# A matmul with leaky ReLU by Strassen's seven products: t2's load issued from another queue, and the last product's two row tiles in two PSUM banks

## The chip, the cores and the metric

The kernel runs on one core of one Trainium2 chip. The metric is device time in microseconds (us); lower is better. Inputs and outputs lie in DRAM.

## The reference

```python
def setup_inputs():
    m, k, n = 4096, 4096, 4096
    return {"a": randn(m, k) as float32, "b": randn(k, n) as float32, "alpha": float32(0.01)}

def reference(a, b, alpha):
    x = np.matmul(a, b)
    return np.where(x > 0, x, alpha * x)
```

## The kernel before

**Tiling.** The output is cut into 4 row groups `g` and 4 column pairs `j`. One pair `(g, j)` is a region of 1024 x 1024 outputs: a 2 x 2 arrangement of blocks of 512 x 512, each 4 row tiles `mt` of 128 rows. The inputs are taken as float16, and the inner dimension is halved too, so that A and B of a region are 2 x 2 blocks (`a11` to `a22`, `B(half, nt, k)`, where `k` counts the two tiles of a half). The first region `(0, 0)` is computed with plain products (line 279). The other 15 are the list `regions`, in the order of the loop at line 715; in groups 1 to 3 the first is `j == CACHED`, column pair 2.

**Seven products.** Each of these regions is computed with seven products instead of eight, by sums of blocks (Strassen's scheme in Winograd's form). `s1` to `s4` are sums of blocks of A (`sum_a`, line 539), `t1` to `t4` sums of blocks of B (`b_sum`, line 569). The products, in order, are a11 x B11, a12 x B21, s2 x t2, s3 x t3, s1 x t4 (written over t2's tiles), a22 x (a sum written over B21), s4 x B22. The text numbers them from 0. Products 0 to 4 are 64 matmuls of 512 columns each (line 734), into four PSUM banks: `y` and `z` in turn. In ten regions the last two products are done by seven quarter products each (`quarter_product`, line 684, 16 matmuls of 256 columns). `keep` (line 747) copies four banks into float32 tiles `c` on ScalarE, `add` (line 864) adds banks to them on VectorE (DVE), and `leave` applies leaky ReLU on DVE (line 307) and stores each tile with a DMA that SyncE (SP) issues (line 869). ScalarE and DVE also measure squares of the inputs (lines 227 to 260), from which the end of the kernel decides whether the result may stand; a branch with a plain product in bfloat16 follows for inputs for which it may not.

**What is kept in DRAM.** A region with `j == CACHED` in groups 2 and 3 finds its sums t2 and t3 ready: group 1's region of the same columns has left them in DRAM tensors `kept_t` (`move_t`, line 500). t3 is loaded during the region before, from `fetch_unit`; t2 is loaded in the region itself, behind product 0, into the tiles with the tag `b11`, the same tiles that held B11 for product 0. Product 2 reads t2. Some loads of B in these regions come from a float16 copy (`kept`, line 510); all other loads of A and B are issued by GpSimd's queue (lines 130 and 513).

**Order.** The instructions of each engine stand in the order in which the code emits them (a manual schedule), with waits on semaphores put in where one engine's work needs another's. Each engine, SP's DMA queue and ScalarE's DMA queue among them, takes its instructions in order; a DMA issue that waits holds back what follows it on its engine. In the first region of groups 2 and 3, SP's order around the change is: four stores of the region before (`leave(kept_c, 0, 1)`), two stores of s2 to DRAM (`keep_s2`, line 707), the two loads of t2 (line 500), four stores of this region's first block. ScalarE's order there is: four copies of the region before (line 1034), four copies of product 0's banks (line 747), later four copies of product 2's. DVE's is: the sums s1 and s2 (line 539), leaky for the stores of the region before, the sums s3 and s4, `add` for product 1.

The place of the load, in the loop over regions:

```python
_, u1 = keep(y, side)
for k in ks:
    if g > 1 and j == CACHED:
        t = have_b[i, k, 0] = b_pool.tile([P, KC, NT], DT, name="b", tag="b11")
        move_t("t2", t, k, False)
        continue
```

**The end.** The seventh product of the last region is `seventh_at_the_end`. Its seven quarter products go partly onto the banks `y`, and partly into two further banks, `one` and `other`. `one` holds two row tiles side by side, 256 columns each. Three quarter products accumulate in it: after the first and the second, ScalarE copies it out (lines 835 and 838); the third, the last of the kernel, is ordered by row tile (`by_row=True`), and DVE adds each half of the bank to both halves of an output tile (line 855), applies leaky, and the tile is stored (line 859, and line 1039 in the branch).

Of the kernel before, what the change touches and what calls it, by code (L numbers as in the profile page):

```python
# [8 lines left out]
P = 128  # L9
DT = mybir.dt.float16  # L10
# [14 lines left out]
KC = 8  # L25
# [5 lines left out]
NT = 512  # L31
# [4 lines left out]
CACHED = 2  # L36
# [10 lines left out]
def kernel(  # L47
# [16 lines left out]
    nc = tc.nc  # L64
# [10 lines left out]
    b_pool = ctx.enter_context(tc.tile_pool(name="bblk", bufs=2))  # L75
# [12 lines left out]
    x = small_pool.tile([P, 8], FP32, name="x")  # L88
# [114 lines left out]
    def new_bank(i):  # L203
        return psum_pool.tile([P, NT], FP32, name="ps", tag=f"ps{i}")
# [98 lines left out]
    part = {}  # L303
    stores = []

    def leaky(t):
        nc.vector.scalar_tensor_tensor(t, t, alpha, t, op0=MULT, op1=MAX if alpha <= 1 else MIN)  # L307
# [27 lines left out]
    for what, i, *more in order:  # L335
        if what == "a":
            r, tiles = more
            k = slice(r * rw, (r + 1) * rw)
# [43 lines left out]
    banks = {}  # L382
# [62 lines left out]
    for i in range(1, len(steps)):  # L445
        t, h, u, first, last = steps[i]
# [16 lines left out]
        t, h, u, first, last = steps[i]  # L463
        if first:
            banks = {(mt, nt): new_bank(2 * mt + nt) for mt in range(MT) for nt in range(2)}
# [18 lines left out]
    kept = dram_pool.tile([2, KU * KW, NT], DT, name="kept")  # L484
# [10 lines left out]
            for k in ks:  # L495
                fetch_unit(i, 2 * half + k, nt)

    def move_t(name, t, k, out):
        ends = kept_t[name][k], t.rearrange("p c n -> p (c n)")
        nc.sync.dma_start(*(ends if out else ends[::-1]))  # L500

    def fetch_unit(i, u, nt):
        g, j = regions[i]
# [15 lines left out]
    have_b = {(0, u, nt): bt[1, u, nt] for u in range(2) for nt in range(2)}  # L519
# [105 lines left out]
    HALF = NT // 2  # L625
# [5 lines left out]
    def a_quarter(t):  # L631
        return t.rearrange("p (c m e) -> p c m e", m=HALF, e=2)

    def b_quarter(t):
        return t.rearrange("p (c n) -> p c n", n=HALF)

    def quarters_of_b(i, half, nt):
        return {(k, n): have_b[i, 2 * half + k, nt][:, :, n * HALF:(n + 1) * HALF]
                for k in range(2) for n in range(2)}

    def quarters_of_a(g, name):
        return {(h, k): operand(g, name, k)[:, :, h * HALF:(h + 1) * HALF, :] for h in range(2) for k in range(2)}
# [32 lines left out]
        for n in which:  # L675
            queue.dma_start(to[n], kept_q[name][n - 1])

    def quarter_product(xq, yq, to, first=False, by_row=False):
        order = [(c, m) for c in range(KC) for m in range(2)]
        if by_row:  # L680
            order = [(c, m) for m in range(2) for c in range(KC)]
        for c, m in order:
            rows = slice(m * P, (m + 1) * P)
            nc.tensor.matmul(  # L684
                to[m], xq[:, c // 2, rows, c % 2], yq[:, c, :],
                start=first and (c, m) == (0, 0), stop=c == KC - 1, skip_group_check=True,
            )

    def into(bank):
        return [bank[:, m * HALF:(m + 1) * HALF] for m in range(2)]  # L690

    def pair(bank):
        return bank.rearrange("p (m n) -> p m n", m=2)
# [21 lines left out]
    for i, (g, j) in enumerate(regions):  # L715

        ks = (1, 0) if in_quarters else (0, 1)
# [5 lines left out]
        zbank = 4 - ybank  # L723
# [15 lines left out]
        def new_c(side):  # L739

            pairs = [c_pool.tile([P, 2, NT], FP32, name="c", tag=f"c{side}") for _ in range(2)]
            return pairs, [pairs[mt // 2][:, mt % 2, :] for mt in range(MT)]

        def keep(banks, side):
            pairs, kept = new_c(side)
            for mt in range(MT):
                nc.scalar.copy(kept[mt], banks[mt])  # L747
            return pairs, kept
# [73 lines left out]
                nc.vector.tensor_add(kept[mt], y[mt], kept[mt])  # L822
            return kept

        def seventh_at_the_end(y, one, other, tq, sq):

            pairs, kept = new_c(side)
            b = quarters_of_b(i, 1, 1)
            x = quarters_of_a(g, "s4")
            t = lambda n: b_quarter(tq[n])  # L830
            sx = lambda n: a_quarter(sq[n])
            block = lambda r, n: pairs[r][:, :, n * HALF:(n + 1) * HALF]
            onto = lambda r, n: [y[2 * r + m][:, n * HALF:(n + 1) * HALF] for m in range(2)]
            quarter_product(x[0, 0], b[0, 0], into(one), True)
            nc.scalar.copy(block(0, 0), pair(one))
            quarter_product(sx(4), b[1, 1], onto(0, 1))
            quarter_product(sx(2), t(2), into(one))
            nc.scalar.copy(block(0, 1), pair(one))
            for mt in (2, 3):
                nc.scalar.copy(kept[mt][:, HALF:], y[mt][:, HALF:])  # L840
            quarter_product(sx(1), t(1), into(other), True)
            nc.vector.tensor_add(block(0, 1), pair(other), block(0, 1))
            nc.vector.tensor_add(block(1, 1), pair(other), block(1, 1))
            quarter_product(x[0, 1], b[1, 0], onto(0, 0))
            even = nc.values_load(good[0:1, 0:1], min_val=0, max_val=1)
            add(kept[:2], y[:2])
            leave(kept[:2], 0, 1)
            quarter_product(x[1, 1], t(4), onto(1, 0))
            for mt in (2, 3):
                nc.scalar.copy(kept[mt][:, :HALF], y[mt][:, :HALF])  # L850
            quarter_product(sx(3), b[0, 1], into(one), by_row=True)
            for mt in (2, 3):
                both_halves = kept[mt].rearrange("p (h n) -> p h n", h=2)
                part = one[:, (mt - 2) * HALF:(mt - 1) * HALF]
                nc.vector.tensor_add(both_halves, part.unsqueeze(1).to_broadcast([P, 2, HALF]), both_halves)  # L855
                leaky(kept[mt])
                last = place(g, 0, mt, j, 1), kept[mt]
                if mt == 2:
                    nc.sync.dma_start(*last)
            return even, last  # L860

        def add(acc, banks):
            for to, bank in zip(acc, banks):
                nc.vector.tensor_add(to, bank, to)  # L864

        def leave(acc, h, nt):
            for mt, t in enumerate(acc):
                leaky(t)
                nc.sync.dma_start(place(g, h, mt, j, nt), t)
# [20 lines left out]
        y = [new_bank(ybank + mt) for mt in range(MT)]  # L890
# [14 lines left out]
            early.end()  # L905
        if middle:
            middle.begin()
        _, u1 = keep(y, side)
        for k in ks:
            if g > 1 and j == CACHED:  # L910
                t = have_b[i, k, 0] = b_pool.tile([P, KC, NT], DT, name="b", tag="b11")
                move_t("t2", t, k, False)
                continue
            b_sum(B(0, 1, k), B(1, 1, k), B(0, 1, k), SUB)
            if late_s2 and k == ks[0]:
                load_s2(g, ks[1], True)
            b_sum(B(0, 0, k), B(0, 1, k), B(0, 0, k), ADD)
            if g == 1 and j == CACHED:
                move_t("t3", B(0, 1, k), k, True)
                move_t("t2", B(0, 0, k), k, True)  # L920
# [32 lines left out]
        if in_quarters:  # L953
            t = x_pool.tile([P, 4, QUARTER], DT, name="q", tag="x")
            tq, sq = {2: t[:, 0], 1: t[:, 1], 4: t[:, 2]}, {4: t[:, 3]}
# [29 lines left out]
        if turning:  # L985
            new_s(g + 1, "s1")
            t = new_s(g + 1, "s2").rearrange("p k c m e -> p (k c m e)").bitcast(BF16)
            a21 = measure(i + 1, 0, 1, 0, t.rearrange("p (n w) -> p n w", n=4))
            a21.begin()
        if in_quarters:  # L990
            tq, sq = sixth_in_quarters(u2_pairs, [new_bank(zbank + mt) for mt in range(MT)], v, y, tq, sq)
# [26 lines left out]
        if in_quarters:  # L1018

            rest = y, new_bank(zbank + 3), new_bank(zbank + 2), tq, sq  # L1020
            if final:
                even, last = seventh_at_the_end(*rest)
            else:
                kept_c = seventh_in_quarters(*rest)
                fetch_b(i + 1, [(1, 1)], (1, 0))
                new_s(g, "s2")
                load_s2(g, 1)
                leave(kept_c, 0, 1)
        else:
            product(6, y, False)  # L1030
            fetch_b(i + 1, [(1, 1)], ks)
            _, kept_c = new_c(side)
            for mt in range(MT):
                nc.scalar.copy(kept_c[mt], y[mt])  # L1034
            leave(kept_c, 0, 1)
# [5 lines left out]
    with inputs.Else():  # L1041
        for m in range(M // RM):
            a_blocks = []
            for u in range(KU):
                t = a_pool.tile([P, KC // 2, RM, 2], BF16, name="a", tag=f"a{u // 2 + 1}{m % 2 + 1}")
                for mt in range(0, MT, 2):
                    to = lambda t0, t1: [t[:, :, (mt + t0) * P:(mt + t1) * P, :]]
# [4 lines left out]
            for n in range(N // NT):  # L1052
                banks = [new_bank(n % 2 * 4 + mt) for mt in range(MT)]
                cols = slice(n * NT, (n + 1) * NT)
                for u in range(KU):
                    t = b_pool.tile([P, KC, NT], BF16, name="b", tag=f"b{u // 2 + 1}{n % 2 + 1}")
                    src = b[u * KW:(u + 1) * KW, cols].rearrange("(p c) n -> p c n", p=P)
                    nc.gpsimd.dma_start(t, src)
                    for c in range(KC):
                        for mt in range(MT):  # L1060
                            nc.tensor.matmul(
                                banks[mt], a_cols(a_blocks[u], c, mt), t[:, c, :],
                                start=(u, c) == (0, 0), stop=(u, c) == (KU - 1, KC - 1),
                            )
                for mt in range(MT):
                    t = c_pool.tile([P, 2, NT], FP32, name="c", tag=f"c{side}")[:, 0]
# [38 lines left out]
```

## Time and profile before

| What | us |
|---|---|
| median of 3 runs | 1555.78 |
| lowest and highest run | 1552.80, 1559.15 |
| the profiled execution | 1562.96 |
| its span, from the first to the last instruction | 1561.10 |
| mean granted TensorE clock | 0.996 |
| TensorE (PE) busy | 1541.8 (99%) |
| DVE busy | 1154.5 (74%) |
| ScalarE (ACT) busy | 373.7 (24%) |
| HBM read and written | 369.10 MB, 98.57 MB |

The profile is of one execution. Its times are in us from the start of its span. A row of a timeline has a start, a length, an engine, a line, the operation with what it writes and reads, a count, and in brackets how long the engine sat idle before it and what released it; an engine name with a q is the queue that issues DMAs. In the rows of waits the figures are the us in total, the number of times and the longest. Rows of PE run on to the end of their last matmul's latency, so consecutive rows overlap a little.

### The profile page before, as it was taken

How to read it: one execution, taken by the hardware profiler on the slowest of the kernel's cores; microseconds unless marked ns; L12 is line 12 of the kernel's file. 1: busy time of each engine (PE TensorE's matmuls, PEld its weight loads, DVE VectorE, ACT ScalarE, POOL GpSimd, SP SyncE). 2: the span in 40 equal slices, each digit the busy share in tenths (PEclk: the TensorE clock that was granted, in tenths of full speed). 3: DMA queues.
4: the chain of work that ended last, by engine and by line, in shares of the span. 5: the costliest groups of instructions: out<-in, count | busy, mean ns of one | idle time of the engine just before them, and what ended most of it. 6: DMA issues, size and time to landing. Idle time of an engine off the chain costs nothing. (4 is left out here: it accounts for less than half of the span.)

```text
span 1561.1 us, 20714 instructions
## 1 busy us (share of the span) xinstructions
PE 1541.8 (99%) x8235; PEld 805.5 (52%) x8235; DVE 1154.5 (74%) x1315; ACT 373.7 (24%) x392; POOL 300.2 (19%) x482
## 2 busy tenths in 40 slices
PE   9999999999999999999999999999999999999997
PEld 4444444444447456474444746547444474745646
DVE  4368758777995686966798588685879668688696
ACT  2201243612100414301211141431021133051430
POOL 5541110244002011023400202012340110201100
PEclk9999999999999999999999999999999999999999
DMA  9999694999869789499987959969998794978923
GB/s 246 186 208 196 138 284 150 184 201 193 283 246 260 166 193 283 122 264 222 182 299 237 245 139 230 229 148 278 208 232 294 189 270 102 275 166 194 288 82 138
DMA packets 210092, 329.68 MB, mean 211 GB/s; under 512 B 18497, under 2 KB 155969, under 8 KB 202050
## 3 DMA queue, kind: packets, MB, share of 16 engines
q0 software_dynamic: 149376, 141.59, 57.1%
q1 hardware_dynamic: 54562, 165.31, 28.4%
q10 hardware_dynamic: 6048, 21.37, 3.7%
q8 instruction: 66, 1.08, 0.3%
q14 instruction: 40, 0.33, 0.1%
HBM read 369.10 MB, written 98.57 MB: 300 GB/s over the span
## 5 line engine op out<-in xcount | busy, mean ns | idle before, releaser
L734 PE MATMUL ps<-b,a 128*128 128x512 f16 x3200 | 696.4, 379 | 0.0
L734 PEld LDWEIGHTS <-a 128*128 128x128 f16 x3200 | 313.0, 98 | 375.7
L734 PE MATMUL ps<-b,s 128*128 128x512 f16 x2240 | 492.1, 381 | 6.6 <-DMA b<-kept_t 6.6
L734 PEld LDWEIGHTS <-s 128*128 128x128 f16 x2240 | 219.8, 98 | 273.6 <-DVE c L864 7.5
L513 POOL DMA_DIRECT2D b<-in_b_dram x184 | 136.4, 746 | 939.0 <-PE ps L734 464.0
L569 DVE TENSOR_TENSOR b<-b 128x4096 f16<-128x4096 f16 x104 | 234.8, 2286 | 94.0 <-DMA b<-in_b_dram 88.0
L747 ACT COPY c<-ps 128x512 f32<-128x512 f32 x180 | 92.6, 597 | 470.8 <-PE ps L734 408.5
L139 DVE STREAM_TRANSPOSE a<-a 128x512 uint32<-128x512 uint32 (+2 forms) x120 | 126.7, 1102 | 82.0 <-DMA a<-in_a_dram 80.5
L130 POOL DMA_DIRECT2D a<-in_a_dram x252 | 137.8, 555 | 195.8 <-DVE a L139 116.4
L307 DVE SCALAR_TENSOR_TENSOR c<-c 128x512 f32<-128x512 f32 x240 | 149.3, 681 | 3.1 <-ACT c L1034 3.0
L227 ACT ACTIVATE sq<-b 128x2048 bf16<-128x2048 f16 x64 | 119.0, 1909 | 106.0 <-DVE sq L236 90.1
L864 DVE TENSOR_TENSOR c<-ps,c 128x512 f32<-128x512 f32 x142 | 88.7, 680 | 74.0 <-PE ps L734 63.2
L684 PEld LDWEIGHTS <-q 128*128 128x128 f16 x1280 | 125.3, 98 | 14.5
L279 PE MATMUL ps<-b,a 128*128 128x512 f16 x512 | 113.1, 379 | 2.7 <-DVE part L318 1.3
L227 ACT ACTIVATE sq<-a 128x2048 bf16<-128x2048 f16 x48 | 89.0, 1908 | 101.1 <-DVE sq L236 80.0
L279 PEld LDWEIGHTS <-a 128*128 128x128 f16 x512 | 49.6, 98 | 64.2 <-issue 5.4
L684 PE MATMUL ps<-b,q 128*128 128x256 f16 x640 | 74.8, 273 | 0.0
L810 ACT COPY c<-ps 128x512 f32<-128x512 f32 x9 | 5.3, 586 | 253.1 <-PE ps L684 140.6
L763 DVE TENSOR_TENSOR c<-ps,c 128x512 f32<-128x512 f32 x80 | 52.2, 683 | 14.6 <-PE ps L684 14.6
L684 PE MATMUL ps<-q,q 128*128 128x256 f16 x480 | 57.3, 273 | 0.0
L684 PEld LDWEIGHTS <-a 128*128 128x128 f16 x480 | 47.0, 98 | 7.6
L684 PEld LDWEIGHTS <-s 128*128 128x128 f16 x480 | 46.9, 98 | 5.5
(101 smaller groups left out, 769.4 us busy)
## 6 DMA issues: line engine op xcount, KB each, us to landing
b<-in_b_dram POOLq DMA_DIRECT2D x192, 512.0 KB, 12.9
out_dram<-c SPq DMA_DIRECT2D x240, 256.0 KB, 6.2
a<-in_a_dram POOLq DMA_DIRECT2D x244, 128.0 KB, 5.4
b<-kept SPq DMA_DIRECT2D x20, 1024.0 KB, 8.3
q<-kept_qs ACTq DMA_DIRECT2D x40, 512.0 KB, 8.2
s<-kept_s SPq DMA_DIRECT2D x18, 1024.0 KB, 7.3
q<-kept_qa SPq DMA_DIRECT2D x28, 512.0 KB, 6.0
b<-kept_t SPq DMA_DIRECT2D x8, 1024.0 KB, 9.2
```

The lines of the kernel that those rows point to most:

```text
L130: nc.gpsimd.dma_start(a16[32 * q:32 * q + 32], src.rearrange("(g i) w -> i g w", i=32))
L139: nc.vector.transpose(part.rearrange("p c m e -> p c (m e)").bitcast(U32) .rearrange("p c (g i) -> p g c i", i=32), src[:, :, i * n:(i + 1 ...
L227: nc.scalar.activation(to, self.parts[n], SQUARE)
L279: nc.tensor.matmul(ps, a_cols(at[0, h, u], c, mt, (h, u) == (0, 0)), bt[0, u, nt][:, c, :], start=first, stop=last,)
L307: nc.vector.scalar_tensor_tensor(t, t, alpha, t, op0=MULT, op1=MAX if alpha <= 1 else MIN)
L513: nc.gpsimd.dma_start(t[:, c:c + 4, :], b_rows(j, u, c, 4, nt, g > 0))
L569: nc.vector.tensor_tensor(f(to), f(x0), f(x1), op)
L684: nc.tensor.matmul(to[m], xq[:, c // 2, rows, c % 2], yq[:, c, :], start=first and (c, m) == (0, 0), stop=c == KC - 1, skip_group_check=True,)
L734: nc.tensor.matmul(banks[mt], a_cols(t, c, mt, t is first_a), B(half, nt, k)[:, c, :], start=first and (k, c) == todo[0], stop=(k, c) == t ...
L747: nc.scalar.copy(kept[mt], banks[mt])
L763: nc.vector.tensor_add(block, pair(t), block)
L864: nc.vector.tensor_add(to, bank, to)
```

## The change

`move_t` gets an argument for the queue, and the two loads of t2 are issued by ScalarE's queue, ahead of the four copies that `keep` puts there, instead of by SP's. In `seventh_at_the_end` the bank `one` is replaced by two banks: each of the two row tiles has the first 256 columns of its own. The new one is `new_bank(zbank + 1)`, which the sixth product's quarters used before. The two copies of a whole bank become two copies of half a bank each, and the adds at the end read the two banks.

```diff
-    def move_t(name, t, k, out):
+    def move_t(name, t, k, out, queue=nc.sync):
         ends = kept_t[name][k], t.rearrange("p c n -> p (c n)")
-        nc.sync.dma_start(*(ends if out else ends[::-1]))
+        queue.dma_start(*(ends if out else ends[::-1]))
...
-    def quarter_product(xq, yq, to, first=False, by_row=False):
+    def quarter_product(xq, yq, to, first=False, by_row=False, banks=1):
...
-                start=first and (c, m) == (0, 0), stop=c == KC - 1, skip_group_check=True,
+                start=first and c == 0 and m < banks, stop=c == KC - 1, skip_group_check=True,
...
-        def seventh_at_the_end(y, one, other, tq, sq):
+        def seventh_at_the_end(y, one, other, tq, sq, one_more):
...
-            quarter_product(x[0, 0], b[0, 0], into(one), True)
-            nc.scalar.copy(block(0, 0), pair(one))
+            ones = [bank[:, :HALF] for bank in (one, one_more)]
+
+            def copies(n):
+                for m in range(2):
+                    nc.scalar.copy(kept[m][:, n * HALF:(n + 1) * HALF], ones[m])
+
+            quarter_product(x[0, 0], b[0, 0], ones, True, banks=2)
+            copies(0)
             quarter_product(sx(4), b[1, 1], onto(0, 1))
-            quarter_product(sx(2), t(2), into(one))
-            nc.scalar.copy(block(0, 1), pair(one))
+            quarter_product(sx(2), t(2), ones)
+            copies(1)
...
-            quarter_product(sx(3), b[0, 1], into(one), by_row=True)
+            quarter_product(sx(3), b[0, 1], ones, by_row=True)
             for mt in (2, 3):
                 both_halves = kept[mt].rearrange("p (h n) -> p h n", h=2)
-                part = one[:, (mt - 2) * HALF:(mt - 1) * HALF]
-                nc.vector.tensor_add(both_halves, part.unsqueeze(1).to_broadcast([P, 2, HALF]), both_halves)
+                nc.vector.tensor_add(both_halves, ones[mt - 2].unsqueeze(1).to_broadcast([P, 2, HALF]), both_halves)
                 leaky(kept[mt])
...
+        have_t2 = g > 1 and j == CACHED
+        if have_t2:
+            for k in ks:
+                t = have_b[i, k, 0] = b_pool.tile([P, KC, NT], DT, name="b", tag="b11")
+                move_t("t2", t, k, False, nc.scalar)
         _, u1 = keep(y, side)
         for k in ks:
-            if g > 1 and j == CACHED:
-                t = have_b[i, k, 0] = b_pool.tile([P, KC, NT], DT, name="b", tag="b11")
-                move_t("t2", t, k, False)
-                continue
+            if have_t2:
+                break
...
-                even, last = seventh_at_the_end(*rest)
+                even, last = seventh_at_the_end(*rest, new_bank(zbank + 1))
```

## The prediction

> **What bounds the kernel now.** I read the page's engine rows first, then the table of waits, then the PE, DVE and SP timelines at the place that the waits name, then the DMA view and the windows there, and last the timeline of the end.
>
> ```profile
> PE 1541.8 (99%) x8235; PEld 805.5 (52%) x8235; DVE 1154.5 (74%) x1315; ACT 373.7 (24%) x392; POOL 300.2 (19%) x482
> ```
> TensorE is the bound: only its gaps are worth anything. The table of waits has one large row of PE's (us in total, times, longest):
>
> ```profile
> PE ps L734 <- DMA b<-kept_t: 6.6, 2, 4.2
> ```
> That is product 2, s2 times t2, of the first region of groups 2 and 3. The three timelines at the first case (start, length, engine, line):
>
> ```profile
> 791.30 27.79 PE L734 MATMUL ps<-b,a 128*128 128x512 f16 x128
> 823.30 15.26 PE L734 MATMUL ps<-b,s 128*128 128x512 f16 x64 [4.21 <-DMA b<-kept_t]
> 838.39 13.98 PE L734 MATMUL ps<-b,a 128*128 128x512 f16 x64
> ...
> 809.88 2.48 DVE L307 SCALAR_TENSOR_TENSOR c<-c 128x512 f32<-128x512 f32 x4
> ...
> 810.58 2.14 SPq L869 DMA_DIRECT2D out_dram<-c  x4
> 812.81 0.89 SPq L707 DMA_DIRECT2D kept_s<-s  x2
> 813.79 2.45 SPq L500 DMA_DIRECT2D b<-kept_t  x2
> ```
> The load of t2 (L500) needs only that product 0 is done with the tile it overwrites. Product 0 began at 791.30 and lasts 13.81 us (the step between two undisturbed product starts, 777.49 and 791.30), so the k=0 tile is free at 798.2 and the k=1 tile at 805.1. But SP issues in order: t2 stands behind four stores of the region before, which wait for leaky on DVE (809.88), and behind two stores of s2. It is issued at 813.79, 15.6 us late, and shares the DMA engines with 3 MB put in just before. The DMA view from 800 to 840 us, one digit per us, and its row for t2 (last figure: us to landing):
>
> ```profile
> DMA  9995200000059999999999998997000069999600
> ...
> b<-kept_t SPq DMA_DIRECT2D x2, 1024.0 KB, 10.0
> ```
> The engines were idle from 805 to 810, ahead of that burst. The second case has the same shape:
>
> ```profile
> 1174.21 27.79 PE L734 MATMUL ps<-b,a 128*128 128x512 f16 x128
> 1204.37 15.66 PE L734 MATMUL ps<-b,s 128*128 128x512 f16 x64 [2.38 <-DMA b<-kept_t]
> 1219.87 13.98 PE L734 MATMUL ps<-b,a 128*128 128x512 f16 x64
> ```
>
> **Part 1, t2 on ScalarE's queue: what goes.** Three products should take 3 x 13.81 = 41.43 us. They took 838.39 - 791.30 = 47.09 and 1219.87 - 1174.21 = 45.66: losses of 5.66 and 4.23, 9.89 together. Of the first, 4.37 is the stall itself (823.30 against a due start of 818.93) and 1.28 follows it; of the second, 2.53 and 1.69. The second piece is the clock. In the windows just behind the stalls (the figure before the last two is the granted clock):
>
> ```profile
> 823.20:826.50 3.30, 3.20 (x9) 1.21 (x10) 3.30 (x6) 0.00 (x0) 0.00 (x0) 0.58 0.93 376
> 1204.30:1208.50 4.20, 4.13 (x12) 1.60 (x13) 4.20 (x6) 0.00 (x0) 0.00 (x0) 0.59 0.96 378
> ```
> The clock was 0.58 and 0.59 there, 1.00 after. The stall took it down, so without the stall both pieces go. The Trainium skill, page "TensorE: Matmul & The Clock Gate", section "What's actually happening", has the array fall to half clock after at least one idle window of about 3.4 us; by that the second stall, 2.4 us, would cost no clock and the sum would be 1.69 less. The trace disagrees: 0.59 behind 2.4 us.
>
> **What it adds.** ScalarE's queue gets two loads behind the copies of the region before (done 792.9) and ahead of product 0's four copies (L747, 804.67). In the built program the loads wait for product 0 and for tile loads of B that were issued before it began, nothing later. An issue on this queue takes 0.33 us (the L676 rows: 0.326 median), so k=0 goes out at 798.2, k=1 at 805.1, and the copies start about 0.8 late and end near 807.6 (in the second case 1181.1, 1188.0 and 1190.5). Behind them nothing runs on ScalarE until 837.95, and product 2 needs the copied banks at 818.93: 11 us of cover, beyond which each us would be a us of stall. Landing: the nearest rows are 4.8 to 10.7 us for L500 and up to 11.2 for the B loads beside it (L510), so k=0 lands by 809.4 (needed 818.93) and k=1 by 816.3 (needed 825.8). Cost: nothing; below nothing is excluded since no consumer starts on the copies before 818.93.
>
> What is late next? Product 2's first weight load then waits for s2 alone, which DVE ended by 809.95 (9 us early). Product 3 needs s3 (816.7) and banks emptied by DVE's L864 (823.54) at 832.7. Product 4 needs t4, from L569, which ran 835.39 to 837.67 for k=0, at 846.6; the k=1 half can only move forward. The quarters that begin at 860.4 need DVE's L646 to L656, done at 851.5. The least of these margins is 8.9 us. Loads of the next region wait on PE's own progress and move with it. Stores on SP only lose two transfers ahead of them. So the 9.89 stays gained.
>
> **Part 2, two banks at the end.** Before, both row tiles of the last quarter product shared a bank, and DVE's add for the first waited for all 16 matmuls:
>
> ```profile
> 1550.76 1.91 PE L684 MATMUL ps<-b,q 128*128 128x256 f16 x16
> 1552.78 0.69 DVE L855 TENSOR_TENSOR c<-ps,c 128x512 f32<-128x512 f32 x1 [1.19 <-PEq L1038]
> ...
> 1554.83 0.69 DVE L307 SCALAR_TENSOR_TENSOR c<-c 128x512 f32<-128x512 f32 x1
> 1555.60 0.33 SPq L1039 DMA_DIRECT2D out_dram<-c  x1
> ```
> Now it waits for the first eight: 8 x 0.109 us earlier (16 matmuls step by 1.75), 0.87. DVE is free then (its last leaky before ended at 1551.59; the add could start at 1551.91) and the copy that it needs ended at 1551.2. The chain add, leaky, add, leaky keeps its lengths, and its second add, at 1553.24, is behind PE's end. All that follows, the last store included, moves by 0.87. Added: each of two copies of 0.59 becomes two of 128x256, 0.66 a pair (L840's row): 0.07 each, under waits for PE of 2.9 us and more. The new bank was last read by the L763 that starts at 1538.72 and is done at 1539.41; its first matmul is due at 1540.39. That cover is 1 us; without it PE would lose what it is short.
>
> **Sum.** 9.89 + 0.87 = 10.76. The profiled execution took 1562.96 (span 1561.10 and 1.86 around it), and would take 1552.20. The median of the runs is 1555.78, 7.18 less than that execution, and PE's steady rate can't be where it differs: from 123.97 to 1552.67 PE lost 10.1 us against its steps, of which 9.89 are these stalls. The 7.18 came from the stalls (9.89), the head (13.5 over its steps), the tail (8.43) or the 1.86, together 33.7. None of it from the stalls: gain 10.76, 1545.0. All of it: 2.71 + 0.87 = 3.58, 1552.2. I take the proportional share, 7.18 x 9.89 / 33.7 = 2.1: gain 8.65, **1547.1**.
>
> **Rivals.**
> - **Small stalls without the profiler.** Stall length hangs on a race of DVE and DMA against PE; it differed by 1.8 us between two equal places. Then the gain is 3.58 to 7.8 and the time 1548 to 1552.2, within 0.5%. For it: the 7.18. Against: no row puts them there. 0.17.
> - **The queue doesn't matter.** If the landing were set by the 16 DMA engines, a load from another queue would land no earlier; only part 2 is left, 1554.9. Against: the idle digits from 805 to 810, and an issue 15.6 us late. The Trainium skill, page "DMA: Bandwidth & Descriptors", section "Issuing engines are not separate DMA queues", says that issuing from several engines saves only the time to initiate; here what is saved is the queue's wait before that. 0.05.
> - **Given back downstream** by a B load or sum I have as covered: half the gain, 1551. 0.04.
> - **Slower: ScalarE is held.** A load that waits on its engine holds the copies behind it. Were the wait for SP's s2 stores (issued 812.81, landing about 820 to 823), t2 would go out at 823 and land at 833: 9.7 us later than now, twice, 1575. It decides from an issue after 813.79. For it: in-order queues caused the present stall. Against: the built waits. 0.08 with lesser forms.
>
> **Numbers.** The forecast has 0.66. About 0.5% (7.8 us) is what a measurement of this kernel tells from no change. Faster by more: 0.66; within: 0.17 + 0.05 + 0.04 = 0.26; slower: 0.08. Range: 1545.0 less 3, half the 6.35 that the runs spread, is 1542; above, 1552.2 and nearly the 1554.9: 1554.
>
> **What would show it.** Right: L500 on ACT's queue at about 798 and 805 (1181, 1188); no PE wait for kept_t; product 2 on time, clock 1.00 behind it; the add at the end about 0.1 us behind the eighth of the last 16 matmuls, not behind the last. Wrong: ACT's L747 later than 817; PE waiting at product 2 for ACT or s2; a new PE wait later in the region; or all of this there and the time within 4 us of before, which would mean the stalls belonged to the profiled execution.

## The result and the profile after

| | kernel before | changed kernel |
|---|---|---|
| median of 17 runs each, us | 1557.99 | 1552.78 |
| lowest and highest run | 1552.80, 1562.46 | 1551.24, 1553.94 |
| the profiled execution | 1562.96 | 1552.24 |

The ratio of the times is 0.9966, with a 95% interval from 0.9957 to 0.9976: faster by 0.34%. The median fell by 5.2 us where 8.65 was forecast, and the profiled execution by 10.72 where the sum said 10.76. The spread of the runs shrank from 9.7 us to 2.7.

The profile after shows the first part as forecast. These are PE's rows at the two places (timeline; start, length, engine, line):

```profile
790.30 27.79 PE L734 MATMUL ps<-b,a 128*128 128x512 f16 x128
817.93 13.98 PE L734 MATMUL ps<-b,s 128*128 128x512 f16 x64
831.74 13.98 PE L734 MATMUL ps<-b,a 128*128 128x512 f16 x64
...
1167.55 27.79 PE L734 MATMUL ps<-b,a 128*128 128x512 f16 x128
1195.18 13.98 PE L734 MATMUL ps<-b,s 128*128 128x512 f16 x64
1208.99 13.98 PE L734 MATMUL ps<-b,a 128*128 128x512 f16 x64
```
Three products take 41.44 us at both places; no wait of PE's for kept_t is left, and the clock stays up (windows behind product 2's start; the figure before the last two is the granted clock):

```profile
817.90:821.00 3.10, 3.10 (x16) 1.42 (x15) 3.10 (x4) 0.00 (x0) 0.00 (x0) 1.00 0.10 42
1195.10:1198.50 3.40, 3.40 (x18) 1.55 (x16) 3.40 (x7) 0.00 (x0) 0.00 (x0) 1.00 0.00 0
```
ScalarE issues t2 at 797.45 and then, once product 0 frees the second tile, again about 7 us later; the copies follow at 804.76 (ACT timeline, and the DMA view's row with the us to landing; this load lands no faster than before, it only leaves earlier):

```profile
797.45 7.19 ACTq L500 DMA_DIRECT2D b<-kept_t  x2
804.76 2.06 ACT L747 COPY c<-ps 128x512 f32<-128x512 f32 x4 [12.85 <-DVE s L539]
```
```profile
b<-kept_t ACTq DMA_DIRECT2D x2, 1024.0 KB, 10.2
```
And the end (timeline):

```profile
1539.89 1.91 PE L684 MATMUL ps<-b,q 128*128 128x256 f16 x16
...
1541.03 0.69 DVE L860 TENSOR_TENSOR c<-ps,c 128x512 f32<-128x512 f32 x1 [0.31 <-PE ps L684]
...
1543.09 0.69 DVE L307 SCALAR_TENSOR_TENSOR c<-c 128x512 f32<-128x512 f32 x1
...
1543.85 0.47 SPq L1047 DMA_DIRECT2D out_dram<-c  x1
```
The first add starts 1.14 us behind the start of the last 16 matmuls, where it was 2.02 before, and the last store is issued 3.96 us behind that start instead of 4.84: 0.88 earlier, as forecast. But the span ends 10.21 us behind the same start, against 10.34 before. Most of the 0.88 does not arrive.

So two questions are left: why the runs gain half of what the profiled executions gain, and where part 2 went.

**A way to add up one execution.** Call S the start of product 0 of the first region of seven products (123.97 before, 122.97 after), and M the start of the last 16 matmuls. Without a stall PE always needs the same from S to M: 1416.92 us in the changed kernel, and within 0.01 of it in the four other profiles without a stall (below). Before, it needed 1550.76 - 123.97 = 1426.79, so its loss is 9.87, the 9.89 of the prediction. What is left of the time is then 1562.96 - 123.97 - 9.87 = 1429.12 before and 1552.24 - 122.97 = 1429.27 after. All experiments below are read with this sum: time = S + loss + about 1429.2, where 1429.2 is the 1416.92 and some 12.3 us behind M. In every profile the losses read off PE's rows at the two places add up to this loss within 0.1 us.

### The profile page after: what moved, and what is told of

The parts are those of the page before. It is cut to its first block, busy times and chain, and to the rows that moved or that the text cites. A ratio compares the mean times of both kernels' runs of the same rounds, so it can differ in the third digit from the quotient of the medians.

```text
span 1550.1 us, 20720 instructions
## 1 busy us (share of the span) xinstructions
PE 1537.9 (99%) x8235; PEld 804.8 (52%) x8235; DVE 1154.6 (74%) x1315; ACT 374.2 (24%) x394; POOL 300.4 (19%) x482
## 4 chain that ended last, share of the span: by engine, by line
PE 96%; DMA 2%; DVE 1%; POOL 1%; issue 1%; ACT 0%; SPq 0%; DVEq 0%
PE ps L734 76%; PE ps L684 16%; PE ps L279 4%; DMA b<-in_b_dram 1%; DVE a L139 1%; DMA a<-in_a_dram 0%; POOL a L130 0%; DMA a_in<-in_a_dram 0%; POOL b L189 0%; DVE part L318 0%; PE turned L366 0%; DVE part L314 0%; DVE c L860 0%; DVE c L307 0%; DVE a L373 0%
## 5 line engine op out<-in xcount | busy, mean ns | idle before, releaser
L139 DVE STREAM_TRANSPOSE a<-a 128x512 uint32<-128x512 uint32 (+2 forms) x120 | 126.8, 1103 | 82.4 <-DMA a<-in_a_dram 79.7
```

Of the source, the lines that this page charges most:

```text
L139: nc.vector.transpose(part.rearrange("p c m e -> p c (m e)").bitcast(U32) .rearrange("p c (g i) -> p g c i", i=32), src[:, :, i * n:(i + 1 ...
```

## The experiments

Times of the runs are medians. Theory A: the stall is a race, and each execution draws another length of it. Theory B: the profiler makes the stall longer. Theory C: the two parts disturb each other.

**Part 1 alone.**

```diff
...
+        have_t2 = g > 1 and j == CACHED
+        if have_t2:
+            for k in ks:
+                t = have_b[i, k, 0] = b_pool.tile([P, KC, NT], DT, name="b", tag="b11")
+                move_t("t2", t, k, False, nc.scalar)
         _, u1 = keep(y, side)
...
```


> Part 1 alone: t2 on ScalarE's queue, the end as before. Theory A (the stalls before product 2 are as long as a race between DVE's chain with SP's stores and PE makes them in that execution; the profiled execution of before, 9.9 us of loss, drew a long pair, and the median run has about 4.3): no PE wait for kept_t, clock 1.00 behind product 2's start, median about 4.3 below before, 1553.6, and a spread of runs like that of the changed kernel (under 3 us, where before has 9.7). Theory B (the profiler makes the stalls longer than they are without it): the same median, but see the rerun of before. Theory C (the two parts overlap or disturb each other, and part 1 alone is worth the full 9.9): 1548.

Measured: 1552.62 us (12 runs, 1551.29 to 1553.61), beside 1557.56 of the kernel before on the same chip (35 runs, 1554.24 to 1564.83); ratio 0.9967 (0.9953 to 0.9981). No loss: S 123.22, M 1540.13, difference 1416.91. The spread is 2.3 us, as A has it; the median is 1 us under A's 1553.6. Part 1 gives all of the changed kernel's gain, and not C's 1548.

**Part 2 alone.**

```diff
...
-            quarter_product(x[0, 0], b[0, 0], into(one), True)
-            nc.scalar.copy(block(0, 0), pair(one))
+            quarter_product(x[0, 0], b[0, 0], ones, True, banks=2)
+            copies(0)
...
-            quarter_product(sx(3), b[0, 1], into(one), by_row=True)
+            quarter_product(sx(3), b[0, 1], ones, by_row=True)
...
```


> Part 2 alone: two banks at the end, t2 on SP as before. Theories A and B: 0.87 us less than before, 1557.1, with the wide spread of before kept; in its profile the first add of the end starts about 0.1 us behind the eighth of the last 16 matmuls, and from the last matmul's start to the last store's issue it is 0.87 us shorter. Theory C: part 2 costs what is missing from the forecast, some 3 us: 1561.

Measured: 1560.43 (12 runs, 1554.94 to 1564.64); ratio 1.001 (0.9992 to 1.0028). No gain shows, and the wide spread stays. The interval does not exclude 0.87 us (0.9992 is 1.2 us less); the kernels with a longer end, below, say more. The median is near C's 1561, but the interval holds 1.000, and by C the changed kernel would be some 3 us slower than part 1 alone, where the two are level (1552.78 and 1552.62); so C falls. In its profile the last store again comes early (3.97 us behind M), and the loss at the two places is 8.44.

**t2 on SP, ahead of the stores.** The four stores of the region before and keep_s2 are emitted behind the loads of t2.

```diff
...
+                move_t("t2", t, k, False)
+            for to, t in held_back:
+                nc.sync.dma_start(to, t)
+            held_back.clear()
+            keep_s2(g)
         _, u1 = keep(y, side)
...
```


> t2 stays on SP's queue, but SP issues it ahead of the four stores of the region before and of the two stores of s2 (these follow it); the end as before. Theory A (what counts is the place in an in-order queue): no PE wait for kept_t, the same time as t2 on ScalarE's queue alone, about 1553.6, and the same small spread. Rival (a queue of its own is what helps, the 2 MB of SP's B loads issued at 796 being ahead of t2 in the same ring): t2 lands later, up to 10 us, but it is needed only at 818.9, so the rival gives a stall only if landing takes over 20 us: 1556 or more.

Measured: 1552.50 (12 runs, 1551.55 to 1554.24); ratio 0.9963 (0.9948 to 0.9977). No loss. Its SP timeline:

```profile
798.00 7.23 SPq L500 DMA_DIRECT2D b<-kept_t  x2
807.89 2.14 SPq L915 DMA_DIRECT2D out_dram<-c  x4
```
The same time as from ScalarE's queue (1552.62), so a queue of its own is worth nothing that these runs show: it is the place in an in-order queue. The Trainium skill's page "DMA: Bandwidth & Descriptors", section "Issuing engines are not separate DMA queues", says that DMAs run on the same 16 DMA engines whichever engine issues them; the two equal times agree. What part 1 removed is the wait ahead of the issue.

**The kernel before, again.**

> The kernel before, unchanged, profiled anew and timed against itself: ratio 1.000. Theory A: this profile shows stalls of another length than 4.4 and 2.5 us, and its span is longer or shorter than 1561.1 by as much as the stalls and their half-clock stretches are. Theory B: the profile again shows about 9.9 us lost at the two places and a span near 1561, whatever the timed runs show.

Measured: ratio 0.9997 (0.9978 to 1.0015); 12 runs from 1553.93 to 1563.93. The profiled one took 1563.30, with a loss of 9.16 that lay elsewhere than in the first profile: its first place lost 1.82 and its second 7.29 (PE timeline, second place, and the end of the stall).

```profile
1171.32 27.79 PE L734 MATMUL ps<-b,a 128*128 128x512 f16 x128
1203.93 16.27 PE L734 MATMUL ps<-b,s 128*128 128x512 f16 x64 [4.82 <-DMA b<-kept_t]
1220.04 13.98 PE L734 MATMUL ps<-b,a 128*128 128x512 f16 x64
```
The length of each stall changes between executions, as A says; the total near 9 fits B as well. This did not yet decide.

**t2 on SP, ahead of the s2 stores alone.** It stays behind the four stores of the region before.

```diff
...
-        if first_of_group and g:
+        if first_of_group and g == 1:
             keep_s2(g)
...
                 move_t("t2", t, k, False)
+            keep_s2(g)
...
```


> t2 on SP, still behind the four stores of the region before, but ahead of the two stores of s2, which follow it; the end as before. Over the six cases profiled so far t2 landed and PE went on 9.3 to 9.5 us behind t2's issue, issued 18.7 to 23.3 us behind product 0's start; product 2 is due at 27.63. Theory A (the stall is issue plus landing less 27.63; the 9.4 of landing hold the 2 MB of s2, about 5 us at 400 MB per ms): issue 1 us earlier and landing about 4 to 5 us faster, so the stall begins only from an issue 23 us behind product 0: almost none is left, median 1552.6 to 1553.5, spread under 4 us. Rival (the landing is latency of the load itself, not its share of the engines): only the 1 us of issue is gained per place, median about 1556.

Measured on a second chip: 1552.42 (7 runs, 1551.58 to 1553.62), beside 1560.78 of the kernel before there (15 runs, 1555.98 to 1565.64); ratio 0.9948 (0.9929 to 0.9967). SP's and PE's rows at the first place:

```profile
813.15 0.89 SPq L500 DMA_DIRECT2D b<-kept_t  x2
814.13 1.17 SPq L707 DMA_DIRECT2D kept_s<-s  x2
```
```profile
790.72 27.79 PE L734 MATMUL ps<-b,a 128*128 128x512 f16 x128
819.38 13.97 PE L734 MATMUL ps<-b,s 128*128 128x512 f16 x64 [0.87 <-DVE s L539]
```
The load was issued 22.4 us behind product 0, as late as in the first profile of before, yet PE went on 6.2 us behind the issue, not 9.5: a stall of 1.03 instead of 4.37, and none at the second place. (The sum named as releaser was long done, by about 810.3; t2 was the last to come.) The first of its two loads, on which PE goes on, landed 6.1 us behind its issue, where it took 9.4 in the first profile of before. The rival (1 us gained per place, 1556) falls: the 2 MB of s2 in front were 3.3 us of t2's landing, somewhat less than the 4 to 5 of Theory A. Moving two stores behind the load brings the whole gain in the runs too, though the issue is as late as ever.

**t2 very late.** It goes behind the stores of product 1's block, so that the stall is long in every execution.

```diff
...
         leave(u1, 0, 0)
+        if have_t2:
+            for k in ks:
+                ...
+                move_t("t2", t, k, False)
```


> t2 on SP behind the four stores of product 1's block too, so that both stalls are long in every run; the end as before. Theory A: issue about 35 us behind product 0's start, landing about 7 later, a stall near 14 us and about 1.7 of half clock at each place, loss some 32 us in the profile and the same in the runs: median about 1584, the profiled execution within 3 us of it. Theory B (a trace overstates what a stall costs a run): the median at least 5 us under the profiled execution.

Measured: 1582.28 (4 runs, 1579.48 to 1584.17), ratio 1.0136 (1.0108 to 1.0165). PE's rows:

```profile
792.24 27.79 PE L734 MATMUL ps<-b,a 128*128 128x512 f16 x128
832.07 16.53 PE L734 MATMUL ps<-b,s 128*128 128x512 f16 x64 [12.04 <-DMA b<-kept_t]
848.44 13.98 PE L734 MATMUL ps<-b,a 128*128 128x512 f16 x64
```
The loss is 30.00 (M 1571.83, S 124.91; A said some 32), and the runs lie 30 us above the kernels without a loss. A us lost in the trace is a us of time. The profiled execution is within 1.9 us of the median, so B's discount of 5 us is not there.

**The changed kernel, and the changed kernel with a longer end.** The second has one more DVE instruction:

```diff
                 leaky(kept[mt])
+                if mt == 3:
+                    nc.vector.tensor_scalar(kept[mt], kept[mt], 1.0, None, op0=MULT)
```


> The changed kernel, unchanged, beside the next one: 1552.7. From the start of the last 16 matmuls to the last DVE instruction's end 3.9 us, as in its first profile.

> The changed kernel with one DVE instruction more at the end: the last output tile is multiplied by 1.0 in place before its store, which puts back 0.4 to 0.7 us of what two banks took from DVE's chain. Theory P (DVE's chain and the last store set the end, and the missing gain of part 2 is noise): 0.4 to 0.7 us longer than the changed kernel beside it, in the runs and from the last 16 matmuls' start to the span's end. Theory Q (something else sets the end at a fixed distance from PE's last product, SP's branch and what follows it): no difference, within 0.2 us.

Measured, beside the same runs of before: 1552.18 (7 runs, ratio 0.9949, 0.9931 to 0.9967) and 1552.65 (8 runs, ratio 0.9952, 0.9936 to 0.9968). The runs can't tell 0 from 0.7. The profiles can, since S and the loss can be taken off. The longer end (timeline; M is 1540.37):

```profile
1543.57 0.69 DVE L307 SCALAR_TENSOR_TENSOR c<-c 128x512 f32<-128x512 f32 x1
1544.29 0.43 DVE L863 TENSOR_SCALAR c<-c 128x512 f32<-128x512 f32 x1
1544.79 0.33 SPq L1049 DMA_DIRECT2D out_dram<-c  x1
```
The last store is issued 4.42 us behind M, against 3.96 in the changed kernel. The whole profiled time less M is 12.41, against 12.35 and 12.21 in the two profiles of the changed kernel, 12.47 in part 2 alone, and 12.14 to 12.48 in eight profiles with one bank, where the last store comes at 4.84. (The ninth with one bank, t2 ahead on SP, has 12.68.) From M to the span's end it is 10.23, against 10.21 and 10.09. So P's 0.4 to 0.7 us are not there and Q's "no difference, within 0.2 us" is: over this stretch the last store does not set the end. But the end isn't at a fixed distance from PE's last product either, as Q has it.

SP's rows show what it does hang on. Behind the last store SP waits until the store before it has landed (L859 before, L864 after: the first of the two row tiles). In all thirteen profiles SP goes on within 0.02 us of that landing and comes to its branch 0.28 us later. With two banks this store is issued 0.88 us earlier too, 2.62 us behind M instead of 3.50, but it takes longer to land (views of the two lines, before and after):

```profile
DMA to landing us min/median/max: 2.5/2.5/2.5
...
DMA to landing us min/median/max: 2.9/2.9/2.9
```
Over the profiles it is 2.3 to 2.6 us with one bank (2.9 in t2 ahead on SP, which explains the 12.68) and 2.9 to 3.2 with two. So SP's branch comes 5.82 to 6.15 us behind M instead of 6.06 to 6.37 (6.72 in t2 ahead on SP), and of the 0.88 some 0.3 is left. The rest of the time, from the branch on, takes 6.32 to 6.53 us with two banks and 5.94 to 6.25 with one, which takes that 0.3 back; nearly all of this growth lies around the span (2.14 to 2.22 against 1.84 to 1.92 in the medians of the runs). The added instruction holds up the last store alone, and so costs nothing. Why the landing and the stretch behind the branch are longer with two banks stays open; a kernel without the branch was not tried.

**Three more draws of the kernel before.**

> The kernel before, unchanged, profiled once more, as another draw of the race. Theory A: time = start of product 0 of the first region of seven products + loss at the two places + 1429.2 us (within 0.4, as in the ten profiles so far); t2 is issued 12.7 to 13.1 us behind the start of the sum s1 on DVE, and PE goes on 9.3 to 9.5 behind that issue; the loss itself may be anything from 0 to 12. Theory B (a profiled execution has the full 9 to 10 us, other runs less): a loss of 8 to 10 again in each of the three draws.

> As the draw before: Theory A the same sum with another loss, Theory B 8 to 10 us again.

> As the two draws before: Theory A the same sum with another loss, Theory B 8 to 10 us again.

Measured, on a third chip: 1558.26, 1557.02 and 1559.68, with losses of 6.15, 4.25 and 6.19 us. Time less S less loss is 1429.06, 1429.37 and 1429.40: the sum holds to 0.2. B falls: a profiled execution may lose 4 us as well as 10. The second draw had no stall at all at its second place (SP timeline, then PE timeline):

```profile
1189.04 2.14 SPq L500 DMA_DIRECT2D b<-kept_t  x2
```
```profile
1172.24 27.79 PE L734 MATMUL ps<-b,a 128*128 128x512 f16 x128
1199.87 13.98 PE L734 MATMUL ps<-b,s 128*128 128x512 f16 x64
1213.68 13.98 PE L734 MATMUL ps<-b,a 128*128 128x512 f16 x64
```
There t2 was issued 16.80 us behind product 0.

Over the twelve places of the six profiles with t2 in its old place (before, part 2 alone, before again and these three) the chain is rigid but for one link. From the start of the sum s1 on DVE to t2's issue: 12.68 to 13.06 us. From the issue to PE's start of product 2, where PE waits for it: 9.3 to 9.5. From product 0's start to the sum s1: anything from 3.8 to 10.4. That is the link that varies, and by the DVE timelines it is loads of A that make it vary. s1 waits for the last transposes of A (L139), and those for the last load of A, 0.94 to 3.55 us at the twelve places. The larger part comes earlier: in the region before, transposes wait for A's loads for 8.1 to 12.8 us in all, and the add behind them (L864 in the kernel before) starts anywhere from 21.7 to 15.7 us ahead of product 0; from there to the six transposes ahead of the last two it is about 14.05 us each time. Why these loads land at other times in each execution is not shown. Product 2 is due at 27.63, so PE stalls whenever t2 is issued later than about 18.2 us behind product 0. Eleven of the twelve were, at 18.7 to 23.3.

## Why the prediction was wrong, and where it was right

- **The bottleneck and the mechanism**: right. t2 stood behind stores in SP's in-order queue, and it could leave as soon as product 0 frees its tile: it did 7.15 us behind product 0's start, where the prediction had 6.9. Part 1 alone and t2 ahead on SP both took the whole loss away. The place in the queue is not all of it, though: the stall is issue plus landing less 27.63, and with the two stores of s2 out of the way of the landing (6.1 us instead of 9.4) a load issued as late as before lost only 1.03.
- **9.89 us of loss in the profiled execution**: right, and worth its full length (t2 very late: 30.00 us of loss, 30 us of time).
- **The step from the profiled execution to the median: wrong. This is the step that failed.** The prediction had 7.18 us between the two and put "the proportional share, 7.18 x 9.89 / 33.7 = 2.1" of it down to the stalls. The other 5.07 it laid to the head, the tail and the 1.86, and took them off the 1552.20 of the profiled execution: 1547.1, which is 5.7 too low. It was nearly all stall. Over all thirteen profiles S varies by 2.0 us (122.89 to 124.91) and what lies behind M by 0.34 in twelve and 0.54 in all, while the loss varied from 4.25 to 9.87 in the six profiles with t2 in its old place. The mean of these six is 7.3, and the profile shown first was the largest. In the comparison of 17 runs the two medians differ by 5.2; with part 2 at nothing that is, as an estimate, the loss of before's median run. Then 4.7 of the 5.0 us between 1562.96 and that median are stall. (The median of the three runs at hand, 1555.78, was itself 2.2 under that of the 17.)
- **The profiled execution fell by 10.72, where the sum had 10.76: luck.** 9.87 of it is the loss and 1.00 an earlier S, less 0.15 behind M; the 0.87 of part 2 is not in it.
- **The rival "small stalls without the profiler"** had the right size (a gain of 3.58 to 7.8; 5.2 came) and named the race. What its name lays to the profiler is not borne out: profiled executions lost 4.25 us as well as 9.87, and where the loss was 30 the profiled one lay within 1.9 us of the median. A lengthening of a us or two is not excluded. "No row puts them there" overlooked the runs: three runs that spread by 6.35 us, on a kernel whose PE is otherwise rigid, were a hint of the race.
- **The size of the gain is no constant**: beside the first chip's runs 5 us, beside the second's 8.4 (ratios 0.9967 and 0.9949 for kernels without a loss), because the kernel before differs (1557.56 and 1560.78), not those without a loss (1552.62 and 1552.18).
- **Part 2's 0.87**: the term was right for the last store's issue and wrong for the end. "All that follows, the last store included, moves by 0.87" failed: the time less M stayed at 12.2 to 12.5. SP's wait for the landing of the store before the last took over half of it back, and the time behind SP's branch the rest.
- **"About 0.5% (7.8 us) is what a measurement of this kernel tells from no change"**: too coarse. The interval, 0.9957 to 0.9976, tells 0.34% from none.
- **What is late next**: nothing, as argued. No PE wait took the place of the old one.
- **The other rivals**: the queue doesn't matter in itself, but the place in it does; ScalarE was not held (copies at 804.76, PE on time); nothing was given back downstream.

## What to carry to other kernels

A stall that comes from a race between two chains is a distribution, and one profile is one draw of it: before costing its removal, profile the kernel several times. The spread of the runs (9.7 to 10.6 us here) says that there is such a race, but not what the median will gain (5 to 8.4). Taking the stall away shows as much in the spread as in the median. A load that is ready early should not stand in a queue behind stores that wait for another engine; which queue it moves to matters less than what stands ahead of it.

## What the runs showed of the hardware that was not expected

The clock fell after gaps of 2.4 us. With t2 in its old place, product 2 starting up to 1.98 us late cost no clock, and from 2.53 us late on it did, 1.3 to 2.9 us each time. Two of the draws show the border: product 2 late by 1.98 and by 2.57 us, PE idle for 1.82 and 2.41 by its rows (windows behind the stall, first and second draw; the figure before the last two is the granted clock):

```profile
819.90:823.30 3.40, 3.31 (x16) 1.57 (x17) 3.40 (x6) 0.00 (x0) 0.00 (x0) 1.00 0.97 390
```
```profile
820.90:824.30 3.40, 3.37 (x9) 1.26 (x10) 3.40 (x6) 0.00 (x0) 0.00 (x0) 0.54 0.94 376
```
The Trainium skill's page "TensorE: Matmul & The Clock Gate", section "What's actually happening", has the clock fall after at least one idle window of about 3.4 us; here 2.4 us were enough, and the measurement decides. Between 1.98 and 2.53 us late there is no case.
